# A two-layer retention and latent-attention trunk: products of zeros at the start, another order for head 0's rotary table, keys and values, and additions to x behind the latent's low parts

## The chip, the cores and the metric

The kernel runs on one core of a Trainium2 chip. The time is the device time of one execution, in microseconds (us). Engines are named as the profile names them: PE is TensorE, DVE VectorE, ACT ScalarE, POOL GpSimd, SP SyncE, which here only issues loads.

## What is computed

The reference takes x (256 tokens by 2048) through two layers in float32:

```
h = rms_norm(x, norm_mix[0])
q, k, v, gate = split(h @ ret_w_in)          # 8 heads: q, k of 256, v and gate of 512
q, k = rope(q), rope(k) * 256 ** -0.5
o = (q @ k.T * decay) @ v                    # chunkwise in the reference, causal
x = x + (silu(gate) * rms(o)) @ ret_w_out
x = x + sq_relu(rms_norm(x, norm_mlp[0]) @ w1[0]) @ w2[0]
# shared keys and values, from a latent of 512 and a rotary part of 64
down = rms_norm(x, kv_norm_in) @ mla_w_kv_down
kv = rms_norm(down[:, :512]) @ mla_w_kv_up
c_q = rms_norm(rms_norm(x, norm_mix[1]) @ mla_w_dq)
q = c_q @ mla_w_uq                           # 16 heads of 128 + 64
x = x + causal_attention(q, kv) @ mla_w_o
x = x + sq_relu(rms_norm(x, norm_mlp[1]) @ w1[1]) @ w2[1]
```

Nearly all of the work is products of the 256 tokens with weights, which are read once from memory (479 MB in all).

## The kernel before

**Products.** Each float32 operand is split into a high part (rounded to fp32r, by ACT, L188 or with a scale L190) and a low part (what is left, by DVE, L189 or L191). A product is then three matmuls: high by high, high by low and low by high (L248 to L250, and L368 to L370). The low part of a chunk of weights thus always passes through ACT first and DVE second, and PE waits for it at its second matmul. Large products are worked as 2 by 2 blocks, some of them with seven instead of eight block products (`quad`, L290, and `gemm_pair`, L345), for which sums of x's blocks are made by `with_sums` (L410 to L412 and their split). `gemm_t` (L257) makes queries and keys in transposed form.

**Weights.** They come in chunks of 1 MB on SP's queue, into three buffers `raw`; high and low parts have five half-chunk buffers each (`wh`, `wl`). Small tiles of 2 KB a partition share a ring of 14 buffers (`f2k`). A new tile of the ring waits until the old user of its buffer is done, the DMAs that read it among them.

**Order.** A clock (`later`, `tick`, `need`, L97 to L112) decides at which point in the stream of chunks each step is written: `later(n, fn)` puts a step n chunks behind, `tick` runs what is due, and `need` runs the queue until a list is filled. A scheduler then fixes each engine's order. `queued_behind(ins, before)` (L283) adds an order without a semaphore.

**The start.** The gate product of head 0 (`rg0`, called at L775 with `start`) takes the first chunks. Ahead of each half-chunk, `first_inputs` (L597) loads two 128-row slices of transposed x (`x0t`) and splits them into `a`. For four slices (`HEAD`) a second load is made later into `x0s` (L611), scaled on ACT (L613) and summed. At the end of this gate `load_x` (L621) loads x in 8 tiles, squares them on ACT, and writes each to its home in memory (`xh`, L628) by POOL's queue. POOL also works through the sine arguments of the rotary table (`sincos`, L511, tiles `tr_...`, then `tm_...` for the second table).

**Head 0.** `scale_tables` (L581) makes x's reciprocal norm `n_r` (L178, POOL), `no_turn` (L584, POOL, a zero that the sine on ACT takes as its bias), the table times the norm (`tr_scaled`), and four transposes into `rope_tab` (L592, due 2 chunks later). Then come the products rq, rk (queries and keys) and rv (values). `ret_rope` (L645) adds up the product, and, after a wait, rotates it on DVE (L656 to L660): 8 - 2 chunks for the queries, 8 - 4 for the keys. `ret_scores` (L665) makes the scores `sc` on PE, and `st`, `sh`, `sl` from them (L677, and the split). `ret_valued` (L737) splits the values into `vh` and `vl`. `ret_out` (L686) multiplies them (`o`, L694), makes `y`, and two chunks later transposes and splits y. The heads 1 to 7 follow the same steps, with values and gate as one pair product (`rp`).

**The latent.** The last product of the first MLP (`d`) ends in `add_to_x` (L486), which adds 512-column blocks to x on DVE (L489, tile `x_mlp`), squares them on ACT, and in `x_block_t` transposes them (`n_tp`), scales and splits them for the latent (`kd`, loop at L893) and for the query's first product (`dqp`). `need(r2, 2)` at L858 draws x's norm, and with it all blocks that it needs, ahead of the first latent product. `downed` (L878) scales the latent's product.

Of the kernel before, what the change touches and what calls it, by code (L numbers as in the profile page):

```python
# [13 lines left out]
BF16 = mybir.dt.bfloat16  # L14
I32 = mybir.dt.int32
AF = mybir.ActivationFunctionType
ALU = mybir.AluOpType
# [18 lines left out]
P = 128  # L36
NT = 2
S = NT * P
D = 2048
KD = D // P  # L40
# [26 lines left out]
def yoco(ctx: ExitStack, tc: tile.TileContext, a):  # L67
    nc = tc.nc
# [23 lines left out]


    queue, low_part, first_low = [], [None], [None]
    clock, count = [0], itertools.count()

    def later(n, fn):  # L97
        queue.append((clock[0] + n, next(count), fn))
# [11 lines left out]
    def need(items, n):  # L110
        while len(items) < n:
            run_first()  # L112
# [10 lines left out]
    nc.gpsimd.memset(neg_half, -0.5)  # L123
    warm = small(1, "warm")
    nc.scalar.copy(warm, neg_half[:, 0:1])

    dram = ctx.enter_context(tc.tile_pool(name="dr", bufs=1, space=bass.MemoryType.DRAM))
    x_home = [[dram.tile([P, 512], F32, name=f"xh_{t}_{b}") for b in range(NB)] for t in range(NT)]
# [81 lines left out]
    def stream(w, chunk, cols, name, use, done=None, before=None):  # L210

        raw = pool.tile([P, 2048], F32, tag="raw", bufs=3, name=f"{name}_raw")
        if before is None:
            nc.sync.dma_start(raw[:, :cols], w[chunk])
        n = cols // 2
        for half in range(2):
            wh = pool.tile([P, 1024], F32R, tag="wh", bufs=5, name=f"{name}_wh{half}")
            wl = pool.tile([P, 1024], F32R, tag="wl", bufs=5, name=f"{name}_wl{half}")
            cuts = 1
            if before is not None:  # L220
                cuts = 1 if half else 2
                m = n // cuts
                for i in range(cuts):
                    lo = half * n + i * m
                    nc.sync.dma_start(raw[:, lo : lo + m], w[chunk][:, lo : lo + m])
                    if i == 0:
                        before(half)
            m = n // cuts
            for i in range(cuts):
                lo = half * n + i * m  # L230
                low_part[0] = split(wh[:, i * m : (i + 1) * m], wl[:, i * m : (i + 1) * m], raw[:, lo : lo + m])
            use(half, wh, wl)
            if half and done is not None:
                queue.append((clock[0] + 0.5, -1, done))
            tick(0.5)
# [250 lines left out]
    def add_to_x(acc, b, ss, name):  # L486
        for t in range(NT):
            for part in acc[t] if isinstance(acc[t], tuple) else (acc[t],):
                nc.vector.tensor_tensor(x[t][b], part, x[t][b], op=ALU.add)  # L489
            if ss is not None:  # L490
                square_sum(x[t][b], ss[1][t][:, b : b + 1], f"{name}_{t}{b}")

# [88 lines left out]
    def scale_tables():  # L581
        r0.extend(x_rstd(ss0, "n0"))
        zero = small(1, "no_turn")
        nc.gpsimd.tensor_scalar(zero, r0[1], 0.0, None, op0=ALU.mult)  # L584
        no_turn.append(zero)
        sc = ret_sc[0](zero)
        scaled = f2k([2, NT, P], "tr_scaled")
        for t in range(NT):
            nc.vector.tensor_scalar(scaled[:, :, t], sc[:, :, t], r0[t], None, op0=ALU.mult)

        def turn():
            nc.scalar.copy(rope_tab, transposed(lambda t, j: scaled[:, j, t], "tr_tp"))  # L592

        later(2, turn)


    act0, sums0, r0, ret_sc, mla_sc, no_turn = [], [], [], [], [], []  # L597
# [25 lines left out]
    def load_x(b):  # L623
        for t in range(NT):
            x0 = f2k([512], f"x0_{t}{b}")
            nc.sync.dma_start(x0, x_in(t, b))
            square_sum(x0, ss0[1][t][:, b : b + 1], f"n0_{t}{b}")
            nc.gpsimd.dma_start(x_home[t][b], x0)  # L628

    def start(half):  # L630
        first_inputs(half)
# [13 lines left out]
    def ret_rope(acc, out, name, wait):  # L645

        u = f2k([2, S], f"{name}_u")
        for i in range(2):
            nc.scalar.copy(u[:, i], acc[i][:, S:])
            nc.vector.tensor_tensor(u[:, i], acc[i][:, 0:S], u[:, i], op=ALU.add)  # L650

        def rotate():
            q = f2k([2, S], f"{name}_q")
            v = f2k([2, S], f"{name}_v")
            cos = rope_tab[:, 1].unsqueeze(1).to_broadcast([P, 2, S])
            nc.vector.tensor_tensor(q, u, cos, op=ALU.mult)  # L656
            for i in range(2):
                nc.vector.tensor_tensor(v[:, i], u[:, 1 - i], rope_tab[:, 0], op=ALU.mult)
            nc.vector.tensor_tensor(q[:, 0], q[:, 0], v[:, 0], op=ALU.subtract)
            nc.vector.tensor_tensor(q[:, 1], q[:, 1], v[:, 1], op=ALU.add)  # L660
            out.append(q)

        later(wait, rotate)
# [22 lines left out]
    def ret_out(h, s, v, gate, y_act):  # L686
        o = two_banks(f"o{h}")
        ys = []
        for t in range(NT):
            for m in range(t + 1):  # L690
                lo = m * S + (t - m) * P
                sh, sl = (i[:, lo : lo + P] for i in s)
                vh, vl = v[m]
                nc.tensor.matmul(o[:, t], sh, vh, start=m == 0, stop=False)  # L694
                nc.tensor.matmul(o[:, t], sh, vl, start=False, stop=False)
                nc.tensor.matmul(o[:, t], sl, vh, start=False, stop=m == t)
        for t in range(NT):
            so = small(1, f"so{h}{t}")
            square_sum(o[:, t], so, f"o{h}{t}")
            ro = rstd(so, RDV, 1, f"o{h}{t}")  # L700
            y = f2k([512], f"y{h}{t}")
            nc.vector.scalar_tensor_tensor(y, o[:, t], ro, gate[t], op0=ALU.mult, op1=ALU.mult)
            ys.append(y)

        def turn():
            for k2 in range(2):
                tp = transposed(lambda t, j: ys[t][:, (2 * k2 + j) * P : (2 * k2 + j + 1) * P], f"ytp{h}{k2}")
                yt = act_tile(f"y{h}{k2}")
                more = None
                if len(y_act) in (HEAD if h < RH // 2 else LATE):  # L710
                    u = f2k([2, S], f"yu{h}{k2}")
                    nc.scalar.copy(u, tp)
                    split_act(yt, u)
                    more = with_sums(u, f"y{h}{k2}")
                else:
                    split_act(yt, tp)
                y_act.append((yt, more))

        later(2, turn)

    ss = square_sums(NB, "ss1")
    act, r = [], []
# [1 line left out]
    halves = [[], []]  # L724

    def ret_projected(h, qk, gate, v, s):

        wait = 0 if h else 8

        def keyed(acc):  # L730
            ret_rope(acc, qk, f"rk{h}", max(wait - 4, 0))
            later(2 if h else 5.5, ret_scores(h, qk, s))

        gemm_t(a["ret_w_qk"], h * 2, act0, KD, f"rq{h}", lambda acc: ret_rope(acc, qk, f"rq{h}", max(wait - 2, 0)))
        gemm_t(a["ret_w_qk"], (RH + h) * 2, act0, KD, f"rk{h}", keyed)

    def ret_valued(src, h, s, v, gate):  # L737
        for t in range(NT):
            vh = f2k([512], f"vh{h}{t}", F32R)
            vl = f2k([512], f"vl{h}{t}", F32R)  # L740
            split(vh, vl, src[t], r0[t])
            v.append((vh, vl))
        later(1 if h else 2, lambda: ret_out(h, s, v, gate, halves[h // 4]))

    def ret_out_half(i):

# [11 lines left out]
    for h in range(RH):  # L758
        qk, gate, v, s = [], [], [], []
        if h == 0:  # L760

            def gated(acc, gate=gate):
                src = [f2k([512], f"gate_raw{t}") for t in range(NT)]
                for t in range(NT):
                    nc.scalar.copy(src[t], acc[t])

                def silu():
                    for t in range(NT):
                        g = f2k([512], f"gate0{t}")
                        nc.scalar.activation(g, src[t], AF.Silu, scale=r0[t])  # L770
                        gate.append(g)

                later(8, silu)

            gemm(a["ret_w_gv0"], 0, act0, KD, 512, "rg0", gated, start)  # L775
            ret_projected(h, qk, gate, v, s)
            gemm(
                a["ret_w_gv0"], 4, act0, KD, 512, "rv0",
                lambda acc, v=v, s=s, gate=gate: ret_valued(acc, 0, s, v, gate),
            )  # L780
            continue

# [72 lines left out]
    ss = square_sums(NB, "ss2")  # L855
    act_kv, act_q, r2 = [], [], []
    mlp(0, act, r, into_next(ss, [G_KV, G_MIX1], [act_kv, act_q], r2, "n2", QUERY))
    need(r2, 2)  # L858


    def pe_rope(dst, u, src, t, i, heads):

# [13 lines left out]
    kpe_t = pool.tile([P, 2, S], F32R, name="kpe_t")  # L876

    def downed(acc, b):  # L878
        for t in range(NT):
            d = f2k([KV_NBS[b]], f"down{t}{b}")  # L880
            nc.scalar.activation(d, acc[t], AF.Copy, scale=r2[t])
            down[t].append(d)
            square_sum(d[:, 0:S], sck[1][t][:, b : b + 1], f"ck{t}{b}")
            if b == 0:
                square_sum(d[:, S:], spe[1][t], f"kpe{t}")
# [331 lines left out]
```

## Time and profile before

| what | us |
|---|---|
| runs shown, median of 3 | 2463.11 (2463.05, 2463.11, 2464.45) |
| profiled execution | 2466.32 |
| its span in the profile | 2464.5 |
| PE busy in the span | 2446.7 |
| PE idle in the span | 17.8 |

The span is the part of the profiled execution that the records cover. In the rows, L12 is line 12 of the kernel before; an arrow `out<-in` names the tiles by the program's names; `x4` is a group of four. In a row of the timeline, the first number is the start from the span's beginning, the second the time to the group's end, and a bracket at the end gives the engine's idle time ahead of it, and what ended this. The duration of a single matmul is longer than the distance to the next one, since matmuls are pipelined. In a row of the waits, the three numbers are the total, how often, and the longest. PEclk is the granted clock of PE, as a share of full speed.

### The profile page before, as it was taken

The numbers are of one execution on the slowest core, as the hardware profiler recorded it, in microseconds if no ns is written. First come the engines' busy times: TensorE is split into PE (matmuls) and PEld (weight loads), VectorE is DVE, ScalarE is ACT, GpSimd is POOL, SyncE is SP. The second block draws the span as 40 slices with busy tenths as digits, with TensorE's granted clock in tenths as the row PEclk, the third lists the DMA queues.
The fourth block names the chain that finished last, engine by engine and source line by source line (L and its number), as shares of the span: only waits on it lengthen the run. The fifth ranks groups of instructions, "written<-read, shape, count | busy, mean of one in ns | idle before, by whom it ended". The sixth has DMA issues, their size and how long they took to land.

```text
span 2464.5 us, 31657 instructions
## 1 busy us (share of the span) xinstructions
PE 2446.7 (99%) x11614; PEld 2062.5 (84%) x11614; DVE 2192.3 (89%) x2894; ACT 1648.4 (67%) x2301; POOL 238.0 (10%) x287
## 2 busy tenths in 40 slices
PE   9999999999999999999999999999999999999999
PEld 7788888888888888888888888998888888888887
DVE  6799899889899999989999998777899999999996
ACT  6566666566677767667676777577676667676673
POOL 7300001000000010010110101101000100100100
PEclk9999999999999999999999999999999999999999
DMA  8555569556565596695785565444565876957864
GB/s 311 195 193 201 177 202 258 198 183 217 200 218 196 199 256 219 207 261 188 245 261 205 187 215 180 154 163 171 179 214 205 247 226 196 262 199 228 264 209 166
DMA packets 93404, 521.04 MB, mean 211 GB/s; under 512 B 11073, under 2 KB 12225, under 8 KB 40001
## 3 DMA queue, kind: packets, MB, share of 16 engines
q1 hardware_dynamic: 71856, 472.83, 55.6%
q0 software_dynamic: 21248, 46.15, 8.8%
q8 instruction: 91, 1.49, 0.3%
q14 instruction: 65, 0.52, 0.1%
q10 hardware_dynamic: 144, 0.05, 0.0%
HBM read 479.14 MB, written 39.85 MB: 211 GB/s over the span
## 4 chain that ended last, share of the span: by engine, by line
PE 94%; POOL 2%; DVE 2%; ACT 1%; DMA 1%; issue 1%; SPq 0%; ACTq 0%
PE u_c L368 7%; PE u_c L370 7%; PE u_c L369 7%; PE d_c L368 6%; PE d_c L370 6%; PE d_c L369 6%; PE rp_c L370 3%; PE rp_c L368 3%; PE rp_c L369 3%; PE u_p L368 2%; PE u_p L369 2%; PE u_p L370 2%; PE rq_acc L276 2%; PE rk_acc L276 2%; PE ro_c L370 2%; PE ro_c L368 2%
## 5 line engine op out<-in xcount | busy, mean ns | idle before, releaser
L189 DVE TENSOR_TENSOR d_wl<-d_raw,d_wh 128x1024 fp32r<-128x1024 f32 (+1 forms) x256 | 280.0, 1114 | 45.6 <-ACT d_wh L188 45.6
L189 DVE TENSOR_TENSOR u_wl<-u_raw,u_wh 128x1024 fp32r<-128x1024 f32 (+1 forms) x256 | 278.8, 1110 | 31.5 <-ACT u_wh L188 31.5
L188 ACT CAST d_wh<-d_raw 128x1024 fp32r<-128x1024 f32 (+1 forms) x256 | 241.8, 975 | 81.3 <-PE d_c L370 38.0
L188 ACT CAST u_wh<-u_raw 128x1024 fp32r<-128x1024 f32 (+1 forms) x256 | 240.7, 971 | 68.4 <-PE u_c L370 33.6
L368 PE MATMUL u_c<-u_wh,n 128*128 128x512 f32 x712 | 277.8, 392 | 0.0
L370 PE MATMUL u_c<-u_wh,n 128*128 128x512 f32 x712 | 277.2, 389 | 0.0
L369 PE MATMUL u_c<-u_wl,n 128*128 128x512 f32 x712 | 277.2, 389 | 0.0
L368 PE MATMUL d_c<-d_wh,hid 128*128 128x512 f32 x660 | 258.4, 392 | 0.0
L370 PE MATMUL d_c<-d_wh,hid 128*128 128x512 f32 x660 | 257.0, 389 | 0.0
L369 PE MATMUL d_c<-d_wl,hid 128*128 128x512 f32 x660 | 256.8, 389 | 0.0
L188 ACT CAST u_wh<-u_u 128x1024 fp32r<-128x1024 f32 x104 | 106.4, 1053 | 106.0 <-DVE u_u L332 66.2
L188 ACT CAST d_wh<-d_u 128x1024 fp32r<-128x1024 f32 x100 | 102.5, 1053 | 96.4 <-DVE d_u L332 60.6
L370 PEld LDWEIGHTS u_c<-u_wh,n 128*128 128x128 f32 x712 | 133.7, 188 | 27.9
L369 PEld LDWEIGHTS u_c<-u_wl,n 128*128 128x128 f32 x712 | 133.8, 188 | 27.1
L368 PEld LDWEIGHTS u_c<-u_wh,n 128*128 128x128 f32 x712 | 133.7, 188 | 27.1
L188 ACT CAST rp_wh<-rp_raw 128x1024 fp32r<-128x1024 f32 x112 | 104.1, 945 | 65.8 <-PE rp_c L370 43.4
L370 PEld LDWEIGHTS d_c<-d_wh,hid 128*128 128x128 f32 x660 | 123.9, 188 | 25.9
L369 PEld LDWEIGHTS d_c<-d_wl,hid 128*128 128x128 f32 x660 | 124.0, 188 | 25.1
L368 PEld LDWEIGHTS d_c<-d_wh,hid 128*128 128x128 f32 x660 | 124.0, 188 | 25.1
L189 DVE TENSOR_TENSOR rp_wl<-rp_raw,rp_wh 128x1024 fp32r<-128x1024 f32 x112 | 119.1, 1084 | 18.2 <-ACT rp_wh L188 18.0
L189 DVE TENSOR_TENSOR u_wl<-u_u,u_wh 128x1024 fp32r<-128x1024 f32 x104 | 123.1, 1217 | 2.3 <-ACT u_wh L188 1.9
L189 DVE TENSOR_TENSOR d_wl<-d_u,d_wh 128x1024 fp32r<-128x1024 f32 x100 | 118.3, 1216 | 0.5 <-ACT d_wh L188 0.5
(566 smaller groups left out, 6571.4 us busy)
## 6 DMA issues: line engine op xcount, KB each, us to landing
u_raw<-in_mlp_w SPq DMA_DIRECT2D x128, 1024.0 KB, 5.4
d_raw<-in_mlp_w SPq DMA_DIRECT2D x120, 1024.0 KB, 4.9
rp_raw<-in_ret_w_gv SPq DMA_DIRECT2D x56, 1024.0 KB, 4.8
ro_raw<-in_ret_w_out SPq DMA_DIRECT2D x32, 1024.0 KB, 5.0
uq_raw<-in_mla_w_uq SPq DMA_DIRECT2D x24, 768.0 KB, 4.5
rq_raw<-in_ret_w_qk SPq DMA_DIRECT2D x16, 1024.0 KB, 4.9
rk_raw<-in_ret_w_qk SPq DMA_DIRECT2D x16, 1024.0 KB, 4.9
xh<-d_c POOLq DMA_DIRECT2D x48, 256.0 KB, 6.1
```

What stands on the lines that cost most here:

```text
L188: nc.scalar.copy(h, src)
L189: return nc.vector.tensor_tensor(l, src, h.bitcast(F32), op=ALU.subtract)
L276: nc.tensor.matmul(acc[f], wh[:, cols], a.rearrange("p i s -> p (i s)"), start=k == 0, stop=k == nk - 1)
L368: nc.tensor.matmul(dst, ah, bh, start=n == 0, stop=False)
L369: nc.tensor.matmul(dst, ah, bl, start=False, stop=False)
L370: nc.tensor.matmul(dst, al, bh, start=False, stop=n == total[key] - 1)
```

## The change

It has three parts. **One**: ahead of everything, DVE sets a tile to zero, and PE multiplies it with itself eight times (bf16, 128x128 by 128x512) into a bank that nobody reads. **Two**: on POOL `n_r` and `no_turn` now come ahead of the 8 writes of x to its home, which are queued behind `no_turn`; the transposes of the rotary table are due 1 chunk later instead of 2; head 0's queries are rotated 8 - 2.5 and its keys 8 - 2.6 chunks later (instead of 8 - 2 and 8 - 4, so the keys later in the program's own count, but with their rotation queued behind the last low part that is written, and the next low part or `vl` behind the rotation); the values are split 1.45 chunks after their product, and `ret_out` follows 0.5 chunks later instead of 2; y of head 0 is turned 3 chunks later instead of 2. **Three**: x's norm is drawn in `downed`, behind the latent's first product, and the adds of the last two blocks of x are queued behind the last low part written before them.

```
+    zeros = pool.tile([P, 512], BF16, tag="junk", bufs=1, name="zeros")
+    nc.vector.memset(zeros, 0.0)
+    idle = bank("acc", [512], "idle")
+    for i in range(8):
+        nc.tensor.matmul(idle, zeros[:, 0:P], zeros, start=i == 0, stop=i == 7)
...
                 low_part[0] = split(wh[:, i * m : (i + 1) * m], wl[:, i * m : (i + 1) * m], raw[:, lo : lo + m])
+                if ahead[0] is not None:
+                    queued_behind(low_part[0], ahead[0])
+                    ahead[0] = None
...
-                nc.vector.tensor_tensor(x[t][b], part, x[t][b], op=ALU.add)
+                added = nc.vector.tensor_tensor(x[t][b], part, x[t][b], op=ALU.add)
+                if name == "n2" and b >= 2:
+                    queued_behind(added, low_part[0])
...
-        nc.gpsimd.tensor_scalar(zero, r0[1], 0.0, None, op0=ALU.mult)
-        no_turn.append(zero)
+        no_turn.extend((zero, nc.gpsimd.tensor_scalar(zero, r0[1], 0.0, None, op0=ALU.mult)))
...
-        later(2, turn)
+        later(1, turn)
...
-            nc.gpsimd.dma_start(x_home[t][b], x0)
+            later(4 - b, lambda t=t, x0=x0: queued_behind(nc.gpsimd.dma_start(x_home[t][b], x0), no_turn[1]))
...
-            nc.vector.tensor_tensor(q, u, cos, op=ALU.mult)
+            turned = nc.vector.tensor_tensor(q, u, cos, op=ALU.mult)
+            if name == "rk0":
+                queued_behind(turned, low_part[0])
...
-            nc.vector.tensor_tensor(q[:, 1], q[:, 1], v[:, 1], op=ALU.add)
+            turned = nc.vector.tensor_tensor(q[:, 1], q[:, 1], v[:, 1], op=ALU.add)
+            if name == "rk0":
+                ahead[0] = turned
...
-        later(2, turn)
+        later(2 if h else 3, turn)
...
-            ret_rope(acc, qk, f"rk{h}", max(wait - 4, 0))
+            ret_rope(acc, qk, f"rk{h}", max(wait - 2.6, 0))
...
-        gemm_t(a["ret_w_qk"], h * 2, act0, KD, f"rq{h}", lambda acc: ret_rope(acc, qk, f"rq{h}", max(wait - 2, 0)))
+        gemm_t(a["ret_w_qk"], h * 2, act0, KD, f"rq{h}", lambda acc: ret_rope(acc, qk, f"rq{h}", max(wait - 2.5, 0)))
...
-            split(vh, vl, src[t], r0[t])
+            low = split(vh, vl, src[t], r0[t])
+            if ahead[0] is not None:
+                queued_behind(low, ahead[0])
...
-        later(1 if h else 2, lambda: ret_out(h, s, v, gate, halves[h // 4]))
+        later(1 if h else 0.5, lambda: ret_out(h, s, v, gate, halves[h // 4]))
...
-                lambda acc, v=v, s=s, gate=gate: ret_valued(acc, 0, s, v, gate),
+                lambda acc, v=v, s=s, gate=gate: later(1.45, lambda: ret_valued(acc, 0, s, v, gate)),
...
-    need(r2, 2)
...
     def downed(acc, b):
+        need(r2, NT)
```

In the order of the instructions this gives, besides: the loads into x0s stand ahead of both loads of head 0's key weights in SP's queue; on DVE the rotation of head 0's keys stands ahead of `vl` and of the keys' own four low parts; in head 1 the rotation of the keys stands ahead of two low parts of y; in the latent the first two low parts, and then three more, stand ahead of the adds of x's last blocks, and PE takes products of the latent's second column block earlier and some of the `n_tp` transposes later.

More of the change, by code (lines that the diff above doesn't have):

```diff
@@ L94, in yoco @@
     queue, low_part, first_low = [], [None], [None]
-    clock, count = [0], itertools.count()
+    clock, count, ahead = [0], itertools.count(), [None]
     def later(n, fn):
```

## The prediction

> **What bounds the kernel now.** I read the summary and the shares of the chain that ended last first, then busy time by stretch, then TensorE's waits.
>
> ```profile
> span 2464.5 us, 31657 instructions
> PE 2446.7 (99%) x11614; PEld 2062.5 (84%) x11614; DVE 2192.3 (89%) x2894; ACT 1648.4 (67%) x2301; POOL 238.0 (10%) x287
> ...
> PE 94%; POOL 2%; DVE 2%; ACT 1%; DMA 1%; issue 1%; SPq 0%; ACTq 0%
> ```
> ```profile
> core 0: us, PE busy (x) PEld busy (x) DVE busy (x) ACT busy (x) POOL busy (x), PEclk, DMA share, GB/s
> 0.00:120.00 120.00, 110.88 (x534) 93.16 (x535) 86.69 (x122) 72.41 (x115) 63.04 (x69) 0.99 0.74 260
> 120.00:1360.00 1240.00, 1240.00 (x5764) 1035.31 (x5763) 1139.49 (x1397) 819.98 (x1057) 83.13 (x117) 1.00 0.66 214
> 1360.00:1450.00 90.00, 87.52 (x481) 75.60 (x480) 81.98 (x140) 68.11 (x132) 8.73 (x11) 1.00 0.61 206
> ...
> 85.00:90.00 5.00, 3.56 (x12) 3.10 (x13) 5.00 (x8) 1.72 (x2) 0.00 (x0) 0.66 0.21 41
> ```
> ```profile
> PE rg_acc L248 <- ACT a L190: 5.4, 1, 5.4
> PE sc L675 <- DVE rk_q L659: 3.7, 2, 2.9
> PE kd_acc L249 <- DVE kd_wl L189: 2.1, 2, 1.2
> ```
> TensorE is busy 99% of the span, and from 120 to 1360 us without a gap (1240.00 of 1240.00): what is won ahead of 120 is kept, and nothing can be won in that stretch. The change removes no product, so it can only gain idle time or a low clock: 120 - 110.88 = 9.1 us in the first stretch, 90 - 87.52 = 2.5 us in the third. The waits name the places: 5.4 us at the start, 3.7 us in two waits of head 0's and head 1's scores on the rotated keys (2.9 and 0.8), 2.1 us in two waits on the latent's low parts. To these comes a low clock: 0.66 of full speed in 85 to 90, right behind the 2.9 us wait, which is 0.34 x 5 = 1.7 us of clock lost. The profiled execution took 2466.32 us (1.8 us outside its span), and the median of the runs is 2463.11: I take gains from the span and subtract them from the median.
>
> **Part 1, the products of zeros.** They can't take away the first 5.4 us, which wait for the first inputs; they can only make the clock full when the real products begin.
>
> ```profile
> 5.41 0.79 PE L248 MATMUL rg_acc<-rg_wh,a 128*128 128x512 f32 x1 [5.41 <-ACT a L190]
> ...
> 10.69 0.63 PE L248 MATMUL rg_acc<-rg_wh,a 128*128 128x512 f32 x1
> ...
> 11.76 0.39 PE L248 MATMUL rg_acc<-rg_wh,a 128*128 128x512 f32 x1
> 11.98 0.39 PE L249 MATMUL rg_acc<-rg_wl,a 128*128 128x512 f32 x1
> ```
> ```profile
> 24.17 2.22 DVE L189 TENSOR_TENSOR rg_wl<-rg_raw,rg_wh 128x1024 fp32r<-128x1024 f32 x1 [0.22 <-ACT rg_wh L188]
> ```
> Before 11.1 us a product of 512 columns shows 0.63 us, after 11.76 0.39, and starts then follow each other by 11.98 - 11.76 = 0.22 us. Between 5.41 and 10.69 lie twelve steps: 5.28 / 12 = 0.44. Some 13 products at 0.44 - 0.22 are 2.8 us lost to the clock. Full speed from the start would pull all 2.8 us forward, if inputs kept up; they don't: at the last group of this gate the low part of the weights ends at 24.17 + 2.22 = 26.39, and products after it can't start earlier by more than about 1 us. Bounds: nothing to 2.8 us inside this stage. The eight products at 0.44 cover 3.5 us and can all lie inside the 5.4 idle. I take 0.9 us at the end of the gate, and nothing of it for the end of the kernel, because the next part shows that head 0 is timed by something else.
>
> By the Trainium skill, page "TensorE: Matmul & The Clock Gate", "Part 1: The HAM clock gate", the clock is raised after a busy window of about 3.4 us and lowered after an idle one, with windows that run freely. By that rule eight products at half speed are barely one window, so whether they warm the clock depends on phase; the trace has both changes, up by 11.76 and down behind 86.44.
>
> **Part 2, head 0.** The idle 2.87 us go away; the question is what is late next. I follow the chain back from the scores.
>
> ```profile
> 56.72 1.68 POOL L547 TENSOR_SCALAR tr_rr<-tr_rr 128x512 f32<-128x512 f32 x1
> 58.36 4.51 POOL L628 DMA_DIRECT2D xh<-x  x8
> 62.88 0.74 POOL L178 TENSOR_TENSOR n_r<-n_m,neg_half 128x2 f32<-128x2 f32 x1
> 63.72 0.24 POOL L584 TENSOR_SCALAR no_turn<-n_r 128x1 f32<-128x1 f32 x1
> ```
> ```profile
> SPq L611 <- DMA xh<-x: 6.1, 1, 6.1
> ```
> ```profile
> 64.48 0.33 SPq L611 DMA_DIRECT2D x0s<-in_xt  x1
> 66.94 0.33 SPq L214 DMA_DIRECT2D rk_raw<-in_ret_w_qk  x1
> 67.31 0.42 SPq L611 DMA_DIRECT2D x0s<-in_xt  x1
> ```
> ```profile
> 75.02 0.91 ACT L613 ACTIVATE x0s<-x0s,gains 128x256 f32<-128x256 f32 x2 [2.65 <-DMA x0s<-in_xt]
> ...
> 75.97 0.43 DVE L410 TENSOR_TENSOR a0s_sum<-x0s 128x256 f32<-128x256 f32 x1 [2.16 <-ACT x0s L613]
> ...
> 80.31 1.40 DVE L191 SCALAR_TENSOR_TENSOR vl<-rv_acc,n_r,vh 128x512 fp32r<-128x512 f32 x2
> ...
> 86.64 3.48 DVE L189 TENSOR_TENSOR rk_wl<-rk_raw,rk_wh 128x1024 fp32r<-128x1024 f32 x3
> 90.05 0.41 DVE L677 TENSOR_TENSOR st<-sc,dec 128x256 f32<-128x256 f32 x1
> ```
> ```profile
> 86.44 2.84 PE L675 MATMUL sc<-rq_q,rk_q 128*128 128x256 f32 x8 [2.87 <-DVE rk_q L659]
> 92.27 0.40 PE L694 MATMUL o<-vh,sh 128*128 128x512 f32 x1
> 110.93 1.32 PE L675 MATMUL sc<-rq_q,rk_q 128*128 128x256 f32 x6 [0.84 <-DVE rk_q L659]
> ```
> ```profile
> 108.84 1.28 DVE L189 TENSOR_TENSOR y<-ytp,y 128x512 fp32r<-128x512 f32 x2
> ```
> The second reload of x (x0s) shares a ring of buffers with the x0 tiles, and SP stood 6.1 us on the first write of x to its home before it could issue the first reload. From the landing of the second (75.02) DVE works without a gap from 75.97 to st at 90.05: 14.08 us. The change reorders these operations (query sums and rotation, key rotation ahead of vl and ahead of the weights' low parts) but the set between landing and st is the same: two rotations, vl, a0s_more and six low parts all still stand ahead of st. So rk_q is ready some 4 us earlier and sc runs then, but st, which the products of o need through sh, stays 14.08 us behind the landing. The landing itself: the writes come 0.74 + 0.24 and a little later on POOL (1.2 us), both reloads now stand ahead of both key chunks in SP's queue (66.94 against 67.31, and a wait of rk_raw on its buffer besides). Bounds for the second landing: 1.2 us later, if the writes alone set it, to 2.5 us earlier, if the queue's order did (67.31 - 64.48 = 2.8). I take 0.3 later, as the 6.1 us wait stays. Then st is at 90.4. In the row of before, sh and o could follow some 1.2 us behind st, but o stood behind the rest of the queries' products until 92.27; now o can start at 91.6, 0.7 sooner. The queries' last low part has four of the keys' (3.48 / 3 = 1.16 each) and one vl (0.7) between itself and st, so it ends at 90.4 - 4.64 - 0.7 = 85.0; its products took 92.27 - (86.44 + 2.84) = 3.0, so TensorE is done at 88.0 and idles 3.6 us until o: a stall in the place of the old one.
>
> For head 1 the order written out on DVE puts the keys' rotation ahead of two low parts of y (1.2 us), so its scores are ready at 110.93 - 1.2 - 0.7 = 109.0. In TensorE's order they stand two products earlier (2 x 0.22), so that 110.48 would equal the old start: 110.48 - 109.0 = 1.45 us are won at 120 if the clock stays full. If the 3.6 us idle lowers it as the 2.87 did, part of o's products runs slow, at a price of up to the same 1.7 us, and about nothing is left. Bounds for this part: 1.45 - 0.9 (landing 1.2 later in place of 0.3) - 1.7 = -1.15, and 1.45 + 0.3 + 2.5 = 4.25. I take 1.1, nearer to the full clock, as the low one ended within 5 us before.
>
> The rest of the edit is hidden: the transposes of the table stand 24 matmuls earlier, 24 x 0.22 = 5.3 us, and POOL's sine chain behind them has no reader before the latent keys. Two copies of the gate stand ahead of one weight copy on ACT (67% busy), at most 0.2 us.
>
> **Part 3, the latent.**
>
> ```profile
> 1405.55 0.68 DVE L489 TENSOR_TENSOR x_mlp<-d_p,x_mlp 128x512 f32<-128x512 f32 x1
> ...
> 1406.76 0.81 DVE L189 TENSOR_TENSOR kd_wl<-kd_raw,kd_wh 128x640 fp32r<-128x640 f32 x1
> ```
> ```profile
> 1405.69 0.45 PE L248 MATMUL kd_acc<-kd_wh,n 128*128 128x320 f32 x2
> ...
> 1407.62 0.42 PE L249 MATMUL kd_acc<-kd_wl,n 128*128 128x320 f32 x1 [0.90 <-DVE kd_wl L189]
> ...
> 1413.27 0.42 PE L249 MATMUL kd_acc<-kd_wl,n 128*128 128x320 f32 x1 [1.21 <-DVE kd_wl L189]
> ```
> ```profile
> 1416.98 0.47 ACT L190 ACTIVATE n<-n_tp,gains 128x256 fp32r<-128x256 f32 x1 [0.54 <-DVE n L191]
> ...
> 1436.97 0.40 PE L368 MATMUL dqp_c<-dqp_wh,n 128*128 128x512 f32 x1
> ```
> The low parts going ahead of the adds removes 0.90 + 1.21 = 2.1 us. In exchange up to four low parts (4 x 0.81 = 3.2 us) stand ahead of the last adds to x, so the transposes of the last blocks (n_tp), their scaling on ACT and the low parts behind them come later, in a serial exchange of ACT and DVE on two banks, in which ACT already waits (0.54). Stepping the new order through with these durations I get new waits of about 0.15, 0.15, 0.7, 1.2 and 0.2 us where products need transposed blocks, 2.4 in all against 2.1 + 0.2 removed, with 0.6 us of other products moved into the gaps: the first query product at 1436.4, 0.5 gained. Bounds: all four low parts on the path, 3.2 lost, to 2.2 gained.
>
> **Sum**: 0 + 1.1 + 0.5, less 0.2 for the gate's copies: 1.4. 2463.11 - 1.4 = **2461.7 us**. The most that all edits could give is 2.8 + 2.87 + 1.7 + 0.84 + 2.2 = 10.4 us, or 0.42%; a measurement of this kernel tells about 0.2%, 4.9 us, from no change.
>
> **Rivals.** (a) *Everything comes through.* If the order in SP's queue set the second landing, it comes 2.5 us sooner, head 0 and 1 give 4.25, the start's 0.9 is kept as DVE no longer holds it back, and the latent gives 1.5: 6.65, or 2456.5. For it: the second reload stands behind a key chunk in the queue. Against it: 6.1 us waiting for the write to its home, which the change makes later. Chance 0.2.
> (b) *A longer wait takes the place of the old in the latent, and the kernel is slower.* If the transposes of the last block wait for all four low parts (3.2 us) and TensorE has run out of latent products, it idles 3.2 more and then works at a low clock as behind 86.44 (1.7): 2463.1 + 4.9 = 2468.0, and with part of head 0's gain 2467. It decides from the point where fewer than 3.2 us of products stand ahead of these transposes; against it speaks that the second column block of the latent stands there and is independent of the late blocks until its fourth chunk. Chance 0.1.
> (c) *Head 0 moves nothing.* The zeros don't raise the clock, or their gain is swallowed, and the 3.6 us idle ahead of o lowers the clock as the 2.87 did, so that what sc wins is given back, and the latent gives little: 2463.0. Chance 0.2. By the clock page of the Trainium skill an idle gap of over about 3.4 us lowers the clock; by that rule (c) has the better half of part 2.
>
> **How the numbers follow.** Forecast 0.5 (its own range 2459.5 to 2463.5), (a) 0.2, (b) 0.1, (c) 0.2. Faster by over 0.2% means under 2458.2: (a) and a little of the forecast's lower end, 0.22. Slower by over 0.2%, over 2468.0: half of (b) and a little, 0.06. Within: 0.72. The range goes from 2456.5, the middle of (a), to 2466.0, the near side of (b), leaving out half of each and some of the unforeseen.
>
> **What would show it.** Start: products at 0.39 us from 5.4 (or still 0.63: the zeros didn't warm). Head 0: sc starting near 83 with no wait, a new wait of some 3.6 us of o on sh, st some 14 us behind the second x0s landing, that landing at 74 to 76, PEclk under 1 behind o's wait or not. Head 1: no wait of sc on rk_q. Latent: no wait on kd_wl, several small ones on n, first query product at 1436.4 less what was won before. I'd be wrong if the second landing moved by over 2 us, if o didn't wait, or if one wait in the latent were longer than 2 us.

## The result: 0.13% slower, and the profile after

The changed kernel takes 2467.82 us (median of 22 runs, 2466.45 to 2470.05) against 2465.09 us for the kernel before in the same measurement (22 runs, 2462.77 to 2467.01). The ratio is 1.0013, with a 95% interval of 1.0007 to 1.0019: slower by 1.7 to 4.7 us, where 1.4 us faster was forecast. That is less than 0.2%, but the interval leaves out no change, and the direction is the other one. The time also lies past the range's upper end of 2466.0. Of these numbers 2.0 us come from the base: the forecast counts from 2463.11, the median of three runs, and the same kernel takes 2465.09 in 22. The 2.7 us between the two kernels are what has to be explained.

The summary and the waits of TensorE in the kernel after:

```profile
span 2466.6 us, 31671 instructions
...
PE 2449.5 (99%) x11622; PEld 2061.6 (84%) x11622; DVE 2195.1 (89%) x2895; ACT 1648.3 (67%) x2301; POOL 237.8 (10%) x287
```
```profile
PE rg_acc L257 <- ACT a L196: 3.3, 2, 2.3
PE o L708 <- ACT sh L194: 3.2, 1, 3.2
PE idle L131 <- DVE zeros L128: 1.2, 1, 1.2
PE sc L689 <- DVE y L195: 1.1, 1, 1.1
...
PE kd_acc L257 <- ACT n L196: 0.8, 1, 0.8
PE n_tp L213 <- ACT n2u L470: 0.6, 1, 0.6
```

The waits that the change was to remove are gone (sc on rk_q, kd_acc on kd_wl). In their place stand o on sh (3.2 us), sc on y (1.1), and two in the latent (0.8 and 0.6); and the gate's products, which have the zeros ahead of them, wait a second time (2.3 us). How far TensorE lies behind the kernel before at five points of its order, from the rows of both timelines:

| point in TensorE's order | before | after | behind |
|---|---|---|---|
| first query product of head 0 | 30.12 | 31.55 | +1.43 |
| first value product of head 0 | 52.70 | 54.47 | +1.77 |
| first product of the latent | 1405.69 | 1407.97 | +2.28 |
| first product of the latent layer's queries | 1436.97 | 1438.70 | +1.73 |
| last product | 2459.71 | 2461.73 | +2.02 |

In this pair of profiles the start loses 1.4 us, the stretch from head 0's values to the latent another half, where 1.1 was to be won, and the 0.55 won at the latent's end is half gone by the last product. One pair misleads, though: the profile of before has a low clock in head 0, which most of its executions don't have, as the experiments show.

**The start** of the kernel after, TensorE's timeline and ACT's (start, duration, and in brackets the idle time ahead and what ended it), and the stretches of 5 us with the clock (PEclk, the third number from the end):

```profile
1.18 3.21 PE L131 MATMUL idle<-zeros 128*128 128x512 bf16 x8 [1.18 <-DVE zeros L128]
...
5.72 0.39 PE L258 MATMUL rg_acc<-rg_wl,a 128*128 128x512 f32 x1
5.95 0.39 PE L257 MATMUL rg_acc<-rg_wh,a 128*128 128x512 f32 x1
...
8.02 0.39 PE L259 MATMUL rg_acc<-rg_wh,a 128*128 128x512 f32 x1
10.74 1.22 PE L257 MATMUL rg_acc<-rg_wh,a 128*128 128x512 f32 x2 [2.34 <-ACT a L196]
...
13.47 0.63 PE L257 MATMUL rg_acc<-rg_wh,a 128*128 128x512 f32 x1
...
31.55 0.61 PE L285 MATMUL rq_acc<-a,rq_wh 128*128 128x512 f32 x2
```
```profile
9.24 1.04 ACT L194 CAST rg_wh<-rg_raw 128x1024 fp32r<-128x1024 f32 x1 [2.95 <-DMA rg_raw<-in_ret_w_gv]
```
```profile
10.00:15.00 5.00, 4.26 (x12) 3.26 (x13) 4.50 (x8) 4.48 (x10) 0.00 (x0) 0.66 1.01 369
```

The zeros do raise the clock here: the first real products follow each other by 0.23 us. But they are the only ones whose inputs are there. TensorE is done with them at 8.4 us, the next half-chunk's cast begins at 9.24, and it idles 2.34 us. Then the inputs are there and the clock is low (0.66 in 10 to 15 us, a product lasts 0.63 us instead of 0.39): full speed while there was little to do, half speed once there was more. In this execution the inputs also came late: the cast began at 8.29 in the profile of before.

**Head 0** after, on POOL, ACT, DVE and TensorE:

```profile
60.53 0.73 POOL L184 TENSOR_TENSOR n_r<-n_m,neg_half 128x2 f32<-128x2 f32 x1 [2.43 <-DVE n_m L183]
61.34 1.18 POOL L595 TENSOR_SCALAR no_turn<-n_r 128x1 f32<-128x1 f32 x1
62.47 4.52 POOL L638 DMA_DIRECT2D xh<-x  x8
```
```profile
75.72 0.91 ACT L623 ACTIVATE x0s<-x0s,gains 128x256 f32<-128x256 f32 x2 [1.65 <-DMA x0s<-in_xt]
```
```profile
76.66 0.65 DVE L419 TENSOR_TENSOR a0s_sum<-x0s 128x256 f32<-128x256 f32 x1 [1.73 <-ACT x0s L623]
...
82.00 0.94 DVE L666 TENSOR_TENSOR rk_q<-rk_u,rope_tab 128x512 f32<-128x512 f32 x1
...
87.12 4.61 DVE L195 TENSOR_TENSOR rk_wl<-rk_raw,rk_wh 128x1024 fp32r<-128x1024 f32 x4
91.66 0.41 DVE L691 TENSOR_TENSOR st<-sc,dec 128x256 f32<-128x256 f32 x1
...
111.99 1.28 DVE L195 TENSOR_TENSOR y<-ytp,y 128x512 fp32r<-128x512 f32 x2
```
```profile
85.18 1.47 PE L689 MATMUL sc<-rq_q,rk_q 128*128 128x256 f32 x8
...
92.86 0.80 PE L708 MATMUL o<-vh,sh 128*128 128x512 f32 x1 [3.23 <-ACT sh L194]
...
112.73 1.57 PE L689 MATMUL sc<-rq_q,rk_q 128*128 128x256 f32 x8 [1.09 <-DVE y L195]
```
```profile
90.00:95.00 5.00, 2.14 (x5) 1.75 (x6) 4.16 (x8) 2.00 (x4) 0.00 (x0) 0.76 1.01 380
```

The scores run 1.3 us earlier (85.18 against 86.44) and are done by 86.6, but st, which multiplies them, stands behind four low parts of head 1's keys (4.61 us) and comes at 91.66, 1.6 later than before. o waits 3.23 us for it and then runs at a low clock.

### The profile page after: what moved, and what is told of

The parts are those of the page before. It is cut to its first block, busy times and chain, and to the rows that moved or that the text cites. A ratio compares the mean times of both kernels' runs of the same rounds, so it can differ in the third digit from the quotient of the medians.

```text
span 2466.6 us, 31671 instructions
## 1 busy us (share of the span) xinstructions
PE 2449.5 (99%) x11622; PEld 2061.6 (84%) x11622; DVE 2195.1 (89%) x2895; ACT 1648.3 (67%) x2301; POOL 237.8 (10%) x287
## 4 chain that ended last, share of the span: by engine, by line
PE 94%; DMA 2%; DVE 2%; ACT 1%; issue 0%; POOL 0%; SPq 0%; ACTq 0%; DVEq 0%
PE u_c L379 7%; PE u_c L377 7%; PE u_c L378 7%; PE d_c L377 7%; PE d_c L379 7%; PE d_c L378 7%; PE rp_c L379 3%; PE rp_c L378 3%; PE rp_c L377 3%; PE u_p L379 2%; PE u_p L377 2%; PE u_p L378 2%; PE d_p L377 2%; PE d_p L378 2%; PE d_p L379 2%; PE rk_acc L285 2%
```

## The experiments

Each kernel is compared with the kernel before, run beside it. Behind the second group stands a table of how many executions of each had a mean granted clock of 1.000 in the records. One low spell, as in the profile of before at 86 to 90 us, costs 1.7 us of clock, or 0.0007 of this mean. Theory 1 or C: the zeros lose. Theory 2 or A: head 0's new order loses, because st still stands behind the four low parts. Rivals are named in each expectation.

**The parts alone.** `zeros_only` is the kernel before with the first hunk of the diff, `head0_only` with part two, `latent_only` with part three, `no_zeros` is the changed kernel without the first hunk.

> The kernel before with only the eight products of zeros. Theory 1 (the full clock makes TensorE use up its first inputs by 8.4 us, it idles some 2.3 us, and the clock falls to half just when inputs are there): slower than before by 1 to 2 us; in the profile a second idle time of the gate's products at about 8.4 to 10.7, a clock of about 0.66 in 10 to 15 us, and the first query product at about 31.5 against 30.12. Theory 2 (the inputs merely landed later in that one profiled execution, and head 0's new order is what loses): no change within 0.5 us, and the first query product near 30.1 or earlier.

> The kernel before with only the second part (head 0's order and the writes of x behind no_turn). Theory 1: the norm is drawn in time again, the second reload lands at about 75, st stands at 90 to 91 and o at about 91.5; faster than before by 0 to 1.5 us. Theory 2: o waits over 3 us on sh and the clock falls behind it, slower than before by 2 us or more.

> The kernel before with only the third part. Both theories: the first query product of the latent layer some 0.5 us earlier behind the end of the MLP (31.0 us instead of 31.28), the two waits on kd_wl gone and about two shorter ones in their place; the time within 1 us of before.

> The changed kernel without the products of zeros. Theory 1: faster than before by 0.5 to 2 us, and about 3 to 4 us faster than the changed kernel, since the start is that of before and parts two and three keep their gains. Theory 2: as the changed kernel, 2 to 3 us slower than before.

| kernel | median us | before | ratio, 95% interval |
|---|---|---|---|
| zeros_only | 2465.65 | 2464.34 | 1.0008, 0.9999 to 1.0017 |
| head0_only | 2467.55 | 2464.34 | 1.0012, 1.0003 to 1.0021 |
| latent_only | 2464.97 | 2464.34 | 0.9999, 0.9991 to 1.0008 |
| no_zeros | 2467.44 | 2464.34 | 1.0013, 1.0004 to 1.0021 |

Theory 1, which I had formed from the two profiles, fell: without the zeros the kernel is as slow as with them, and the interval of `zeros_only` includes no change. Part two by itself carries the loss; in its profile o waits 3.23 us on sh and the clock is low behind this, as theory 2 said. In the profile of `latent_only` the first query product comes 1434.36 - 1403.56 = 30.80 us behind the latent's first product, against 31.28, as forecast.

**What in part two.** `st_first`: the changed kernel without the zeros, and every low part of head 1's keys queued behind st:

```
+                if st0[0] is not None and name.startswith("rk1"):
+                    queued_behind(low_part[0], st0[0])
...
+            if h == 0:
+                st0[0] = last
```

The first lines stand in the function that splits the chunks, the last ones in `ret_scores`, where `last` is the second operation on st.

`fill_o`: the changed kernel without the zeros, with 20 transposes of the unit matrix into o's bank ahead of o's products. `writes_only`: the kernel before with only the two hunks on `no_turn` and `x_home`. `turns_only`: part two without these.

> The changed kernel without the zeros, and with the four low parts of head 1's keys queued behind st of head 0 on DVE. Theory A (head 0 loses because st still stands behind four low parts, so that o waits 3.2 us, and the clock falls behind this wait in nearly every execution): the wait of o on sh is gone or under 0.6 us, o starts some 3 us sooner (near 88 to 89), the clock of the executions is mostly 1.000, and the time is 2460 to 2463, 1 to 4 us faster than before. Theory B (head 0 loses because its inputs come later: the second reload, or POOL's later work beside DVE): no more than 1 us better than without this edit, 2466 or more.

> The changed kernel without the zeros, with 20 transposes of the unit matrix (into o's bank, overwritten by o's first product) between the queries' last product and o, so that TensorE isn't idle there; o itself is as late as without them. Theory A1 (of head 0's loss, 1.5 us or so is the low clock behind the wait): about 1 to 2 us faster than without the transposes, near 2466, and the clock of the executions mostly 1.000. Theory A2 (the wait alone is the loss): no change, near 2467.4.

> The kernel before with only the order on POOL changed: the writes of x to its home behind no_turn. Theory A: the second reload lands within 1 us of before, the time is within 1 us of before. Theory B: the second reload lands 1 us later or more, DVE's chain to st runs beside POOL's second sine chain, the time 1 to 3 us slower than before.

> The kernel before with the rest of the second part: table, rotations, values, o in the new order, the writes as before. Theory A: o waits over 3 us on sh, clock mostly 0.999, 2 to 3 us slower than before. Theory B: within 1 us of before or faster.

| kernel | median us | before | ratio, 95% interval |
|---|---|---|---|
| st_first | 2463.09 | 2464.73 | 0.9996, 0.9987 to 1.0005 |
| st_first_again | 2462.64 | 2464.73 | 0.9993, 0.9984 to 1.0002 |
| fill_o | 2466.25 | 2464.73 | 1.0008, 1.0000 to 1.0017 |
| writes_only | 2465.80 | 2464.73 | 1.0006, 0.9997 to 1.0015 |
| turns_only | 2465.91 | 2464.73 | 1.0005, 0.9996 to 1.0014 |

One order on DVE takes the ratio from 1.0013 to 0.9996 and 0.9993, 4 to 5 us. In the profile of `st_first`, DVE, TensorE and the stretches:

```profile
84.67 0.41 DVE L687 TENSOR_TENSOR st<-sc,dec 128x256 f32<-128x256 f32 x1
85.00 0.27 DVE L688 TENSOR_TENSOR st<-sc,dec 128x128 f32<-128x128 f32 x1
85.20 1.21 DVE L189 TENSOR_TENSOR rk_wl<-rk_raw,rk_wh 128x1024 fp32r<-128x1024 f32 x1
```
```profile
87.20 0.40 PE L706 MATMUL o<-vh,sh 128*128 128x512 f32 x1
```
```profile
85.00:90.00 5.00, 5.00 (x28) 4.24 (x27) 5.00 (x9) 2.17 (x4) 0.00 (x0) 1.00 0.78 247
90.00:95.00 5.00, 5.00 (x31) 4.35 (x30) 3.52 (x5) 2.33 (x6) 1.73 (x4) 1.00 0.96 374
```

TensorE has no gap from 85 to 95, and o starts at 87.20 without a wait. So st's place behind the four low parts is what holds o, as theory A says, and theory B's 2466 or more did not come. But the kernel before has the same low parts ahead of st. Their place explains why nothing was won, not yet why the new order is slower than the old. In `fill_o` the transposes fill the gap but for 1.04 us, and o is as late as without them:

```profile
88.10 2.35 PE L700 MATMUL o<-cst 128*128 128x128 f32 x20
91.49 0.50 PE L709 MATMUL o<-vh,sh 128*128 128x512 f32 x1 [1.04 <-ACT sh L188]
```

| kernel | executions at clock 1.000 | of | mean time at 1.000, us | mean time below, us |
|---|---|---|---|---|
| before | 72 | 99 | 2464.2 | 2465.7 |
| after | 2 | 22 | 2466.9 | 2468.2 |
| head0_only | 0 | 11 | | 2467.5 |
| no_zeros | 2 | 11 | 2466.0 | 2467.7 |
| fill_o | 10 | 11 | 2466.3 | 2467.9 |
| st_first, twice | 17 | 22 | 2463.2 | 2463.4 |
| writes_only | 7 | 11 | 2465.4 | 2466.5 |
| turns_only | 6 | 11 | 2464.9 | 2466.9 |
| zeros_only | 6 | 11 | 2465.5 | 2466.4 |

With the wait of 3.2 us on sh, nearly no execution keeps the full clock (2 of 22 in `head0_only` and `no_zeros`; in after, a spell at the start can add to this); with the gap filled, 10 of 11 do. From `no_zeros` to `fill_o` the ratio falls from 1.0013 to 1.0008, about 1.2 us, though these two intervals overlap. A1 stands by the clock's count. But the low clock is the smaller part of the loss. A low spell costs 1.5 us in the kernel before and 1.7 in `no_zeros`, and it comes in 27 of 99 executions against 9 of 11: about 0.9 of the 3.1 us between their medians. At full clock the new order is still some 2 us slower (2466.0 in two executions of `no_zeros`, 2466.3 in ten of `fill_o`, against 2464.2).

`writes_only` and `turns_only` are each some 1 us slower than before, and no change lies within either interval: the halves of part two are not told apart. `turns_only` is not what theory A expected: o waits 2.36 us, not over 3, and 6 of 11 executions keep the full clock. In `writes_only` the second reload is scaled at 74.66, within 1 us of before.

To put head 0 in numbers of its own: the stretch from its first value product to the latent's first product holds the same work in all kernels. It is 1351.5 us on the mean of eight profiles with the order of before (1349.6 to 1353.0), 1353.5 in five with the order of after (1352.8 to 1354.0), and 1348.9 in three with st first (1348.5 to 1349.9). The new order costs 2.0 us, and st first would have won 2.6. The same profiles show where the 2.0 lie. In the five with the new order o starts 1.20 or 1.21 us behind st. It does so too in each of the five with the old order whose clock is full up to there; in the three with a low clock it is 2.22, because the scores and the products behind them run slowly. `latent_only` has the old order:

```profile
88.67 0.41 DVE L679 TENSOR_TENSOR st<-sc,dec 128x256 f32<-128x256 f32 x1
```
```profile
89.88 0.50 PE L696 MATMUL o<-vh,sh 128*128 128x512 f32 x1 [0.47 <-ACT sh L188]
```

So st held o already in the old order, with TensorE's idle time mostly ahead of the scores. The change moves this idle time behind them, in one piece, and frees nothing at o. In fact o comes 1.0 us later, 38.7 us behind the first value product on the mean (38.2 to 39.7) instead of 37.7 (35.6 to 39.6). So does the second reload, scaled 21.9 us behind that product (21.3 to 23.2) instead of 20.9 (19.2 to 22.3). Whether the moved writes delay it or chance does is not shown, so theory B, of later inputs, may have a part of some 1 us. The other 1.0 lies behind o. From o to the latent's first product seven of the eight profiles of the old order take 1313.4 to 1313.8 us (`zeros_fill` 1315.1), the two of the new order with a full clock 1314.1 and 1314.2, and the three with a low one 1315.0 to 1315.5.

**Control, a filled start, an earlier reload.** `before_again` is the kernel before, unchanged. `zeros_fill` adds to `zeros_only` seven more zero products behind the first half-chunk. `x0s_early` is `st_first` with the first two reloads of x in tiles of another ring:

```
-                again = f2k([2, S], f"x0s_{c}")
+                again = act_tile(f"x0s_{c}", F32)[:, 0] if c in (2, 4) else f2k([2, S], f"x0s_{c}")
```

> The same kernel as st_first, run again for a narrower interval and a second profile. Theory A: 1 to 3 us faster than before again, no wait of o on sh. If the first result was chance: within 0.5 us of before.

> The kernel before, unchanged, as a control and for a second profile. No difference beyond 1 us in the time. If the low clock behind the wait of the scores is what the first profile had and most executions do not: the clock here is 1.00 in 85 to 90 us, with the scores' wait on the rotated keys between 1.5 and 2.9 us.

> The kernel before with the eight products of zeros, and seven more zeros behind the products of the first half-chunk, so that TensorE isn't idle while it waits for the second. Theory C (the zeros lose because TensorE, at full clock, runs out of inputs and the clock falls in that gap): the clock stays 1.00 in 5 to 15 us, the first query product comes at 29 to 30, and the time is 1 us or more below that of the zeros alone (2465.7), at or under before. Theory D (the start is set by the landing of the inputs, whatever the clock): the first query product at 30 or later, and the time as with the zeros alone.

> As st_first, with the first two reloads of x in tiles of another ring, so that their loads don't wait for the writes of x to its home. Theory E (the landing of the second reload sets head 0): it lands 2 us sooner or more (under 72), st stands at 83 or sooner, and the time is 1 to 2 us below st_first, near 2461 to 2462. Theory F (TensorE's own products set head 0 once st stands ahead): no change against st_first beyond 0.5 us.

| kernel | median us | before | ratio, 95% interval |
|---|---|---|---|
| before_again | 2464.34 | 2464.73 | 1.0001, 0.9992 to 1.0010 |
| zeros_fill | 2464.95 | 2464.73 | 1.0002, 0.9993 to 1.0011 |
| x0s_early | 2462.12 | 2464.73 | 0.9990, 0.9981 to 0.9999 |

`before_again` has the kernel before's time. In its profile the scores wait 2.15 us and the clock is low behind this too (0.66 in 85 to 90 us), so the first profile was no single case; by the table it is the rarer one. `x0s_early` beats both kernels, and all of its 11 executions keep clock 1.000. But it doesn't decide between E and F: only the first reload came earlier (scaled at 64.66), the second stands behind a key chunk in SP's queue and was scaled at 73.64, not under 72, and its gain on `st_first` is inside the intervals. `zeros_fill` decided nothing either: in its profile the zeros had not raised the clock when the real products began, and the filling zeros only took their time.

**The start again.** Four single profiles, on how often the zeros raise TensorE's clock in time and whether the loads land later with them.

> The zeros alone, a further look at the start. If the zeros make the loads land later: the third cast of the gate's weights on ACT at 9.0 us or later. If that was chance: at 8.1 to 8.8 us as in ten of eleven profiles without zeros. If the clock's windows run by themselves: the first real products at a step of 0.23 in some executions and 0.43 in others.

> The zeros alone once more, another execution. If the zeros make the loads land later: the third cast of the gate's weights on ACT at 9.0 us or later; if chance: at 8.1 to 8.8 us.

> The changed kernel again. If the zeros make the loads land later: third cast at 9.0 us or later, and the first query product near 31.5; if chance: 8.1 to 8.8 and near 30.

> The changed kernel without the zeros again: third cast at 8.1 to 8.8 us, first query product at 29.6 to 30.8; o waits 3.2 us on sh, as in the first profile of it, with the clock low behind it in this execution or not.

`zeros_look1` and `zeros_look2` are the same kernel:

```profile
1.18 3.33 PE L131 MATMUL idle<-zeros 128*128 128x512 bf16 x8 [1.18 <-DVE zeros L128]
...
5.66 0.39 PE L255 MATMUL rg_acc<-rg_wl,a 128*128 128x512 f32 x1
5.89 0.40 PE L254 MATMUL rg_acc<-rg_wh,a 128*128 128x512 f32 x1
...
10.50 0.88 PE L254 MATMUL rg_acc<-rg_wh,a 128*128 128x512 f32 x2 [2.13 <-ACT a L196]
```
```profile
1.18 3.60 PE L131 MATMUL idle<-zeros 128*128 128x512 bf16 x8 [1.18 <-DVE zeros L128]
...
6.15 0.63 PE L255 MATMUL rg_acc<-rg_wl,a 128*128 128x512 f32 x1
6.58 0.63 PE L254 MATMUL rg_acc<-rg_wh,a 128*128 128x512 f32 x1
```

In three of six profiles with zeros (after, `after_look`, `zeros_look1`) the real products began at full speed. In all three TensorE then idled 1.6 to 2.3 us, the clock read 0.66 in 10 to 15 us, and head 0's first query product came at 31.1 to 31.6. In the other three it came at 30.2, 30.9 and 31.3 (the last with the filling zeros), and in twelve profiles without zeros at 29.6 to 30.8, but for one at 31.5. So the zeros win nothing sure, and where they come in time the query product is about 1 us later. How much of this is their own is open, because the third cast (the one shown at 9.24) was late in these profiles: it began at 8.6 to 9.2 in the three, at 8.4 to 9.1 in the other three, and at 8.1 to 8.8 without zeros, but for one at 9.3. This one, `st_first_again`, has the 31.5, as late as any with zeros. Whether zeros delay the loads stays open too.

## Why the prediction was wrong, point by point

- **The start.** "Bounds: nothing to 2.8 us" left out the loss. I reckoned that inputs would limit the gain, and didn't follow what a TensorE that outruns its inputs does next: it idles, and the clock falls in that gap. The first query product came 1.43 us later here, but so did its inputs by 0.95 (the third cast at 9.24 against 8.29), so the price of the fallen clock alone isn't known. For the end of the kernel the term was 0, and that held: with and without the zeros the ratio is 1.0013. The sentence on the phase of the clock's windows (the Trainium skill, "TensorE: Matmul & The Clock Gate", "Part 1: The HAM clock gate": windows run freely, so the point of change depends on where the first product falls) fits the two profiles above, one at full speed and one not, though no run shows the windows themselves. That a whole idle window is needed to lower the clock does not fit: gaps of 1.6 to 2.3 us did.
- **"The landing ... I take 0.3 later."** 0.7 later here (75.72 against 75.02). In the eight profiles of the old order it is 72.95 to 75.02, 74.05 on the mean, and in the five of the new one 74.20 to 76.54, 75.42 on the mean: the term was probably too small by about 1 us, though some executions of either order agree. I had overlooked that `n_r`, moved ahead, waits for DVE's `n_m`: POOL stood 2.43 us, and the writes left 4.1 us later than before, not 1.2. Nor did "both reloads now stand ahead of both key chunks" come true. SP's rows after have the order of before, a chunk between the reloads (it belongs to head 1's keys, and so do the low parts that "The change" calls the keys' own):

```profile
65.10 0.33 SPq L621 DMA_DIRECT2D x0s<-in_xt  x1
65.52 0.40 SPq L220 DMA_DIRECT2D rk_raw<-in_ret_w_qk  x1
66.75 0.33 SPq L621 DMA_DIRECT2D x0s<-in_xt  x1
```

  The second reload was issued 0.56 us sooner than before and scaled 0.70 later.
- **"st stays 14.08 us behind the landing."** The mechanism was right. The 14.08 counts from DVE's first operation on the reload; counted so, it is 15.00 here (76.66 to 91.66). Operations on DVE were longer while POOL's second sine chain, now later, ran beside them (rk_q 0.94 us against 0.68); that the one makes the other is argued, not tested.
- **"TensorE now idles some 3.6 us: a stall in the place of the old one."** Right: 3.2 us, in five of five profiles with the whole of part two's order.
- **"now o can start at 91.6, 0.7 sooner" and "I take 1.1, nearer to the full clock."** This is the step that failed: head 0's term of +1.1, where the stretch lost 2.0. The 0.7 is the distance by which o followed st in the one profile of before, 2.22 us, less the 1.2 that it needs and 0.3 for the landing. That distance was a mark of this execution's low clock. At full clock o follows st by 1.2 us in the old order too, so with st left in its place nothing was to be won there, and o came 1.0 later. The clock is the second fault. I had it in the sum's lower bound (-1.15) and took a value near the full clock, because before's low clock ended soon. It is a matter of how often: by their mean clock 27 of 99 executions of before have a low spell, 9 of 11 of `no_zeros` and all 11 of `head0_only`. By the times above the clock makes about 0.9 us of the loss, and some 2 us stay without it.
- **"its scores are ready at 110.93 - 1.2 - 0.7 = 109.0."** Wrong in kind. Head 1's scores use one of two banks that y's transposes hold until y's low parts have read them. Putting the rotation ahead of these only changed the name of the wait: sc waits 1.09 us on y, where it waited 0.84 on rk_q. So none of the 1.45 us that were to be won at 120 came.
- **The latent, "0.5 gained".** 0.55 at the first query product, by two waits of 0.83 and 0.55 us of the expected kind. But it is given back: from the latent's first product to the last of the kernel, nine profiles with part three take 1054.0 us on the mean and nine without it 1053.9. The transposes of the rotary keys now stand behind that first query product and wait 0.38 us themselves. I had ended my sum at a point that the change had also moved.

The rival that came nearest is (c): head 0 moves nothing because its new wait lowers the clock. What it lacked is that before pays for a low clock in only a quarter of its executions and the new order in nearly all, and that o isn't sooner even at full clock. The slower rival (b) names 2467 to 2468, where the time lies, but that is luck: the longest wait in the latent is 0.83 us, not 3.2.

## What to carry to other kernels

When a wait on the critical path goes because its operation is put ahead, look at what the consumer of *its* result stands behind. Here the scores were freed and st was left where it was, and one more order (st ahead of four low parts) took the kernel from 0.13% behind before to some 0.05% ahead of it, an amount that the intervals can't tell from no change, and with the earlier reload to 0.10% ahead. End a sum only at a point that the change doesn't move. Ask of more than one profile whether its clock is the usual one before reading distances off it, and count a low clock by how often it comes: in 27 of 99 executions of before, whose scores wait 2.15 and 2.87 us in its two profiles, and in 20 of 22 with a wait of 3.2 us.

## What the runs showed of the hardware

- The clock of TensorE can fall after gaps of 1.6 to 2.3 us at the start and of 2.2 to 3.2 us in head 0, and can stay full after 2.7 (`zeros_only`) and 3.2 (`no_zeros`, both profiles). The low spell lasts some 3.4 us (at half clock, from 1.7 us of clock lost), in `after_look` twice that, and products of 512 columns are then 0.43 us apart instead of 0.23.
- The granted clock in the records doesn't show the slow products at the very start: it reads 1.00 in 5 to 10 us of the kernel before, where products of 512 columns are 0.43 us apart too.
- The landing of the same first loads differs between executions by up to 1.3 us (the third cast at 8.06 to 9.31 us), and the end of the first gate follows it: 29.55 us for the earliest, 31.46 for the latest of the profiles without zeros. This alone is 0.08% of the time.
